# The order of the side work in a diffusion transformer step: new tables for a kernel on one core, with DMA transposes kept apart from GpSimd transfers

## The chip, the cores and the metric

The kernel runs on one core of a Trainium2 chip. The time is that of one execution on the device in microseconds, the median of 3 runs; beside it stands one profiled execution with its trace. The engines are named as in the profile: PE (matmuls), PEld (their weight loads), DVE (VectorE), ACT (ScalarE), POOL (GpSimd) and SP (SyncE, which here only issues DMAs).

## The reference

One layer of a hybrid diffusion backbone, for two groups of 128 tokens (context tokens and latent tokens), in float32 with d = 2048 and a hidden width of 8192:

```
sh1, sc1, g1, sh2, sc2, g2 = split(silu(cond) @ w_ada + b_ada, 6)
h  = rms_norm(x) * (1 + sc1) + sh1
qa, ka, va, qb, kb, vb, ga, gb = split(h @ w_in)
oa = window attention (qa, ka, va);  ob = neighbourhood attention (qb, kb, vb)
x  = x + g1 * ((sigmoid(ga) * (oa @ w_br_a) + sigmoid(gb) * (ob @ w_br_b)) @ w_out)
h2 = rms_norm(x) * (1 + sc2) + sh2
x  = x + g2 * (relu(h2 @ w_up) ** 2 @ w_down)
```

The new keys and values are outputs too. Both groups use the same weights, so each weight tile is multiplied with two sets of 128 tokens (s = 0 and 1).

## The kernel before, in words

**Steps.** The work of PE is a list of 456 steps. A step takes one weight tile of 128x1024 float32 (512 KB) and does 12 matmuls of 512 columns with it. A float32 product is made of three: a value is split into a high part, rounded to the matmul's format, and a low part, the rest; the three products are high x high, low x high and high x low (lines 323 to 325, 434 to 436, 1117 to 1119, 1295 to 1297). The steps in order: 72 for the first projections (q, k, v of both mixers), 64 for the two gates, 32 for the branches (w_br_a and w_br_b, `br_unit`), 32 for w_out (`out_unit`; the last of its four units, out unit 3, is `split_unit`, lines 1089 and on), 16 for the first two units of w_up, and then 7 times 16 steps of w_up in pairs (`up_pair`, steps x and y, with sums of two tiles in place of a part of the products) and 16 of w_down for each pair (`down_unit`).

**What happens to a weight tile.** SP loads it into `raw` (line 231). ACT rounds it to `wH` (`copy`, line 103). DVE subtracts, `wL = raw - wH` (line 265). For the steps listed in `LO_DMA` the low part is made without DVE: ACT writes -wH into `wL` (line 271), and POOL issues a DMA that reads the tile from memory once more and adds it there (line 272, an accumulating transfer). In the pair steps the same is done for `XL`.

**Side work.** Beside that the engines do:

- *Dots* (`dot`, line 1522): the columns of the modulation and of the gates, as products of a row of w_ada with the condition, summed along the row, on DVE. There are 288 such instructions of 128x1024, each followed by a short read-out of its sum; the rows `aT` are loaded by SP (line 1509).
- *Attention*: 8 jobs of logits, softmax and products. Line 891 is the low part of an attention output.
- *Transposes by DMA*: the merged branches m (units 0 to 2) and the activations a of w_up. ACT parts the float32 tile into two planes of 16 bits (`part`, `plm`, `pla`), SP issues a DMA transpose (`flip`, line 953, to `pTm`, `pTa`), ACT puts the planes together (`join`, `fTm`, `fTa`) and rounds (`m2H`, `a15H`), and DVE subtracts (`m2L`, line 976). Unit 3 of m is transposed on PE (`m3H`, `m3L`, line 933).
- *Residuals* (`resid`, lines 1067 and 1068), running sums of w_down (`dsum`, brought back into the accumulators by ACT, `acc<-dsum`, at the start of a unit), and the rows of the gates.

**What sets the order.** Nothing is scheduled by a planner when the kernel is built: the program is written out step by step (`run`, line 293 and on), and each engine works through its own instructions in the order of the program. Tables say at which step each piece of side work is written: `RUN` (a digit for each step: how many steps ahead loads are issued on SP beyond their own lead of 4 steps), `HIA` and `LOOK` (how many steps ahead of PE a tile is rounded and subtracted), `LO_DMA`, `DOTS1`, `DOTS` and `DOTS2` (the steps of the dots), `POST` and `JOBS` (the projections' post-processing and the attention), `M_AT` (for m: the steps after a branch unit at which it is parted, flipped and joined), `U_AT` (the nine pieces of work on each activation a), and some smaller ones. The loop of `run`:

```
while loads and loads[0][0] <= st["i"] + int(RUN[st["i"]]):
    loads.pop(0)[2]()
...
to = st["i"] + int(LOOK[st["i"]]) + 1
while by_dma and by_dma[0] < to + LO_AHEAD:
    ...
    lo_dma(wsteps[by_dma.pop(0)])
prep_to(to, int(HIA[st["i"]]))
st["mm"](st)
```

Of the kernel before, what the change touches and what calls it, by code (L numbers as in the profile page):

```python
# [41 lines left out]
GATE_BACK = 6  # L42
SEED_IN = {3: -1, 4: 0}
SEED_N = (1, 2, 3)
HIA = "334344422101100011100000000122301011111222111222166947553425111013333021221100230021210000200214411000472412200014311212000122441111340010000000100122421210000000000001112224211011355330120500215121100112110022235222103132111122441101022101040213137010043200000101443744564163220000103331003200200112443223211311333897310001332111426411523212022201234110234223000000000021732332243121010110011213659743433000051332322214785182125200100010143210114545247413"
JOIN_LO = 0
SEED_AT = 3
LATE = [1, 0, 0]
ROW_AT = [5, 7, 9, 5]
DIRECT = (3,)  # L50
LO_DMA = [61, 64, 67, 72, 77, 86, 91, 97, 103, 106, 107, 113, 123, 125, 132, 140, 152, 154, 158, 172, 177, 184, 189, 193, 197, 201, 202, 204, 215, 218, 222, 224, 226, 228, 230, 239, 247, 260, 278, 288, 292, 294, 302, 305, 309, 328, 342, 348, 354, 356, 362, 365, 368, 371, 376, 382, 386, 390, 406, 414, 418, 425, 435, 446, 448, 449]
LO_AHEAD = 2

LOOK = "611111122363415244252311332123001130322324232612423111125313141113103124074704401120241642343511333310300011222612060000014948241210105200123253889630426264732454425776691438524821000552257766731000423585037723000160012257691101111014410471447943352966841121000121002032123342233698754699677424411101024267483385777010270111001021431214537842533637352231110241333343187810360357244476465534430140000167275946725442541264301421633233599410002355000466876767"
RUN = "121456457242233512302534211343337663233346434536220000101365356572666431264421250221316831178776544354000102511343588636956330015435499665668999887888323637578788887648731488478895889530499775199482898837126887976459874624247999999989999999999999978377888242565341101001446688446069336899993237667668533532789985978888888888888889987999988889898688615227566656714569888889886476735635451169947788986689998899999999999987898787999999856889995561687444265000"
CONST_AT = [47, 44, 82, 62, 99, 93]
ADA_AT = [None, 5, 13, 22, 24, 38]
XS_AT = {1: 11, 2: 1, 3: 23}
POST = {('kvA', 0): [56, 63, 78], ('qA', 0): [54, 58, 69], ('qA', 1): [67, 70, 79], ('kB', 0): [68, 70, 76], ('qB', 0): [74, 85, 95], ('kB', 1): [86, 104, 106], ('qB', 1): [98, 98, 105]}
JOBS = [[84, 85, 85, 90, 102], [81, 83, 84, 98, 111], [82, 89, 95, 102, 111], [86, 98, 106, 109, 111], [103, 105, 109, 116, 122], [103, 104, 108, 110, 123], [108, 109, 116, 124, 128], [113, 113, 116, 124, 127]]  # L60
SS_AT = [74, 74, 128, 139]
T_AT = [3, 4]
PREP_IN = [5, 7]
DOTS = [49, 51, 52, 52, 53, 56, 57, 57, 59, 59, 61, 63, 66, 69, 69, 70, 70, 77, 80, 80, 81, 82, 82, 83, 83, 85, 85, 85, 89, 89, 90, 92, 92, 96, 99, 99, 99, 101, 101, 104, 104, 106, 106, 108, 108, 109, 109, 110, 112, 113, 114, 119, 119, 121, 121, 121, 121, 125, 125, 128, 128, 130, 131, 132, 136, 136, 137, 137, 137, 140, 140, 146, 149, 149, 150, 150, 153, 153, 155, 156, 163, 167, 171, 171, 172, 174, 175, 175, 179, 180, 184, 186, 186, 187, 188, 190]
DOTS2 = [235, 236, 237, 266, 268, 271, 299, 301, 331, 331, 333, 363, 363, 365, 397, 397, 424, 430, 430, 430, 430, 430, 431, 433, 440, 440, 440, 440, 443, 444, 444, 444]
STAT_AT = [4, 2, -1, 8]
U_AT = [[[1, 2, 5, 10, 10, 15, 15, 21, 22], [2, 10, 13, 14, 16, 17, 19, 23, 25]], [[7, 10, 12, 13, 13, 21, 22, 28, 30], [11, 13, 14, 14, 15, 16, 22, 29, 31]], [[6, 7, 9, 9, 11, 26, 28, 28, 30], [13, 22, 22, 22, 22, 31, 33, 33, 33]], [[6, 8, 8, 9, 10, 12, 14, 14, 16], [3, 5, 5, 5, 5, 11, 23, 26, 32]], [[0, 4, 4, 7, 12, 25, 30, 30, 30], [4, 4, 4, 6, 6, 12, 20, 28, 31]], [[2, 2, 2, 2, 2, 16, 25, 26, 28], [2, 9, 9, 9, 11, 21, 24, 31, 32]], [[8, 8, 9, 9, 9, 10, 11, 11, 11], [2, 8, 9, 9, 10, 13, 13, 13, 16]]]
# [12 lines left out]
def tile_hybrid_step(ctx: ExitStack, tc: tile.TileContext, a):  # L80
# [209 lines left out]

    by_dma = sorted(LO_DMA)

    def run():
        loads.sort(key=lambda x: x[:2])
        for st in wsteps:
            while loads and loads[0][0] <= st["i"] + int(RUN[st["i"]]):
                loads.pop(0)[2]()
            for j in sorted(j for j in pre if j <= st["i"]):
                for fn in pre.pop(j):
                    fn()  # L300
            to = st["i"] + int(LOOK[st["i"]]) + 1
            while by_dma and by_dma[0] < to + LO_AHEAD:
# [156 lines left out]
    def mod_pair(f):  # L459

        box, k0 = {}, 2 * f
        i = ADA_AT[f]
        for j in range(2):
# [310 lines left out]

    for u, ps in POST.items():
        nh = 2 if u[0] == "kvA" else 4
# [230 lines left out]
    def br_unit(n):  # L1007
# [195 lines left out]
    def up_unit(n):  # L1203
# [514 lines left out]
```

## Time and profile before

| | |
|---|---|
| median of 3 runs | 1311.11 us (1310.46 to 1311.5) |
| profiled execution | 1309.16 us |
| its span in the trace | 1307.4 us |
| instructions of PE, DVE, ACT, POOL | 6074, 1609, 1364, 130 |
| granted clock of PE over the span | 0.998 |
| read from memory, written | 403.87 MB, 14.99 MB |

The span runs from the first instruction to the last one; 1.8 us of the execution's time lie outside it. A row of a timeline gives start, duration, engine, line, operation, the tile written and the tiles read, the shape, and in square brackets how long the engine stood idle before it and what released it. A matmul's duration is modelled, and matmuls overlap, so their distance is read from the starts.

### The profile page before, as it was taken

The numbers are of one execution on the slowest core, as the hardware profiler recorded it, in microseconds if no ns is written. First come the engines' busy times: TensorE is split into PE (matmuls) and PEld (weight loads), VectorE is DVE, ScalarE is ACT, GpSimd is POOL, SyncE is SP. The second block draws the span as 40 slices with busy tenths as digits, with TensorE's granted clock in tenths as the row PEclk, the third lists the DMA queues.
The fourth block names the chain that finished last, engine by engine and source line by source line (L and its number), as shares of the span: only waits on it lengthen the run. The fifth ranks groups of instructions, "written<-read, shape, count | busy, mean of one in ns | idle before, by whom it ended". The sixth has DMA issues, their size and how long they took to land.

```text
span 1307.4 us, 18070 instructions
## 1 busy us (share of the span) xinstructions
PE 1286.4 (98%) x6074; PEld 1044.6 (80%) x6074; DVE 1216.4 (93%) x1609; ACT 963.6 (74%) x1364; POOL 107.7 (8%) x130
## 2 busy tenths in 40 slices
PE   8999999999999999999999999999999999999998
PEld 4777788888878888877887887888888888888876
DVE  4589999989999999899789999999999989999997
ACT  5534778967857555655888887898889888888771
POOL 0000002202300000000101000000000010010010
PEclk9999999999999999999999999999999999999999
DMA  9999999999999999999599979899899899999995
GB/s 371 408 409 409 405 363 346 375 335 385 273 367 355 379 378 348 312 360 376 156 271 288 379 238 357 240 330 341 272 351 238 306 305 297 341 279 337 395 321 193
DMA packets 158572, 431.07 MB, mean 330 GB/s; under 512 B 53088, under 2 KB 54352, under 8 KB 158480
## 3 DMA queue, kind: packets, MB, share of 16 engines
q1 hardware_dynamic: 145264, 383.39, 79.5%
q0 software_dynamic: 13024, 46.44, 16.8%
q8 instruction: 47, 0.77, 0.2%
q14 instruction: 45, 0.37, 0.1%
q10 hardware_dynamic: 192, 0.10, 0.0%
HBM read 403.87 MB, written 14.99 MB: 320 GB/s over the span
## 4 chain that ended last, share of the span: by engine, by line
PE 74%; DMA 14%; DVE 6%; ACT 4%; issue 2%; ACTq 0%; DVEq 0%; SPq 0%
PE acc L324 12%; PE acc L323 12%; PE acc L325 12%; PE Q L1296 5%; PE Q L1297 5%; PE Q L1295 5%; PE acc L434 5%; PE acc L435 5%; PE acc L436 5%; DMA raw<-in_w_out 3%; DMA aT<-in_w_adaT 3%; DMA raw<-in_w_in 2%; DMA araw<-in_w_pair 1%; PE ps_ada L340 1%; DVE wL L265 1%
## 5 line engine op out<-in xcount | busy, mean ns | idle before, releaser
L103 ACT ACTIVATE wH<-raw 128x1024 fp32r<-128x1024 f32 (+1 forms) x347 | 347.5, 1044 | 105.8 <-DMA raw<-in_w_in 27.9
L265 DVE TENSOR_TENSOR wL<-raw,wH 128x1024 fp32r<-128x1024 f32 x294 | 346.1, 1220 | 11.1 <-ACT wH L103 10.2
L434 PE MATMUL acc<-wH,hH 128*128 128x512 f32 x276 | 108.7, 394 | 0.7 <-ACT u_qB L103 0.7
L435 PE MATMUL acc<-wL,hH 128*128 128x512 f32 x276 | 107.6, 390 | 0.0
L436 PE MATMUL acc<-wH,hL 128*128 128x512 f32 x276 | 107.5, 389 | 0.0
L323 PE MATMUL acc<-wH,hH 128*128 128x512 f32 x256 | 102.3, 399 | 0.0
L325 PE MATMUL acc<-wH,hL 128*128 128x512 f32 x256 | 99.8, 390 | 0.0
L324 PE MATMUL acc<-wL,hH 128*128 128x512 f32 x256 | 99.8, 390 | 0.0
L1522 DVE CUSTOM_DVE_ANT_0 junk<-aT,cB,cols 128x1024 uint8<-128x1024 f32 x72 | 92.5, 1285 | 0.9
L1522 DVE CUSTOM_DVE_ANT_0 aT<-aT,cB,cols 128x1024 f32<-128x1024 f32 x72 | 91.3, 1294 | 0.3
L103 ACT ACTIVATE uH<-raw 128x1024 fp32r<-128x1024 f32 x56 | 58.9, 1052 | 17.8 <-DVE raw L1367 14.1
L1361 DVE TENSOR_TENSOR t<-raw 128x1024 f32<-128x1024 f32 x56 | 68.2, 1217 | 3.4 <-PE acc L324 3.4
L1373 DVE TENSOR_TENSOR tL<-t,tH 128x1024 fp32r<-128x1024 f32 x56 | 68.2, 1218 | 2.5 <-ACT tH L103 2.1
L1373 DVE TENSOR_TENSOR uL<-raw,uH 128x1024 fp32r<-128x1024 f32 x56 | 68.2, 1217 | 0.2
L103 ACT ACTIVATE XH<-raw 128x1024 fp32r<-128x1024 f32 x56 | 58.7, 1050 | 7.1 <-DVE uL L1373 2.6
L103 ACT ACTIVATE tH<-t 128x1024 fp32r<-128x1024 f32 x56 | 58.8, 1049 | 6.5 <-DVE t L1361 3.3
L434 PEld LDWEIGHTS acc<-wH,hH 128*128 128x128 f32 x276 | 51.8, 188 | 13.7 <-issue 2.1
L436 PEld LDWEIGHTS acc<-wH,hL 128*128 128x128 f32 x276 | 51.8, 188 | 10.9
L435 PEld LDWEIGHTS acc<-wL,hH 128*128 128x128 f32 x276 | 51.8, 188 | 10.7 <-DVE wL L265 0.3
L325 PEld LDWEIGHTS acc<-wH,hL 128*128 128x128 f32 x256 | 48.1, 188 | 10.1
L323 PEld LDWEIGHTS acc<-wH,hH 128*128 128x128 f32 x256 | 48.1, 188 | 9.5 <-issue 0.2
L324 PEld LDWEIGHTS acc<-wL,hH 128*128 128x128 f32 x256 | 48.2, 188 | 9.4 <-DVE scT L1522 0.2
(668 smaller groups left out, 3476.0 us busy)
## 6 DMA issues: line engine op xcount, KB each, us to landing
raw<-in_w_in SPq DMA_DIRECT2D x133, 512.0 KB, 10.2
raw<-in_w_down SPq DMA_DIRECT2D x128, 512.0 KB, 10.2
raw<-in_w_upF SPq DMA_DIRECT2D x112, 512.0 KB, 6.2
aT<-in_w_adaT SPq DMA_DIRECT2D x80, 512.0 KB, 10.2
aT<-in_w_gT SPq DMA_DIRECT2D x64, 512.0 KB, 10.2
araw<-in_w_pair SPq DMA_DIRECT2D x48, 512.0 KB, 10.2
raw<-in_w_out SPq DMA_DIRECT2D x32, 512.0 KB, 10.8
XL<-in_w_upF POOLq DMA_DIRECT2D x19, 512.0 KB, 8.8
```

The source lines that it names most:

```text
L103: act.activation(out, in_, AF.Copy)
L265: dve.tensor_tensor(st["lo"], st["raw"], st["hi"].bitcast(F32), op=OP.subtract)
L323: pe.matmul(acc[tb], sh, wh[:, k, :], start=f, stop=False, **kw)
L324: pe.matmul(acc[tb], sh, wl[:, k, :], start=False, stop=False, **kw)
L325: pe.matmul(acc[tb], sl, wh[:, k, :], start=False, stop=l, **kw)
L434: pe.matmul(acc[tb], sh, wh[:, k, :], start=kt == 0 and k == 0 and not held and not seeded, stop=False, **kw)
L435: pe.matmul(acc[tb], sh, wl[:, k, :], start=False, stop=False, **kw)
L436: pe.matmul(acc[tb], sl, wh[:, k, :], start=False, stop=last and k == 1 and not hold, **kw)
L1295: pe.matmul(acc, stat[0], hi, start=f, stop=False)
L1361: dve.tensor_tensor(t.rearrange("p (a n) -> p a n", a=2), X.rearrange("p (a n) -> p a n", a=2), Y[:, 0:512].unsqueeze(1).to_broadcast([P, ...
L1373: dve.tensor_tensor(b[n + "L"], v, b[n + "H"].bitcast(F32), op=OP.subtract)
L1522: dve.tensor_tensor_reduce(out, box["raw"], cB[s, tag], 1.0, dst if second else baT[:, part, fb:fb + 1], OP.mult, OP.add, dst)
```

## The change

The change alters tables alone; no function and no line of the code behind them. Line 36 (`DOTS1`), line 45 (`HIA`), line 51 (`LO_DMA`, 65 entries where there were 66) and lines between 54 and 74 hold new numbers. A cut of the diff:

```diff
-DOTS1 = [12, 12, 19, 21, 21, 24, 27, 28, 32, 32, 34, 37, 37, 38, 38, 40]
+DOTS1 = [16, 17, 17, 19, 21, 27, 28, 32, 33, 34, 34, 38, 38, 38, 40, 40]
...
-M_AT = [1, 6, 9]
+M_AT = [2, 6, 10]
 FLIP = 2
-P_UP = [3, 0]
+P_UP = [2, 0]
...
-STAT_AT = [4, 2, -1, 8]
+STAT_AT = [2, 0, -1, 8]
```

`HIA`, `LOOK`, `RUN`, `LO_DMA`, `DOTS`, `DOTS2`, `POST`, `JOBS`, `CONST_AT`, `ADA_AT`, `XS_AT` and `U_AT` are replaced as a whole. Over the program PE has the same instructions in the same order. The subtractions of wL on DVE go from 294 to 297 and those of XL from 37 to 35; the accumulating transfers for wL of w_br_a go from 2 to 3, of w_br_b from 2 to 1, of w_out from 6 to 5, of w_down from 18 to 17, of w_up from 4 to 3, and those for XL from 19 to 21. The digits of `RUN` for steps 20 to 59 sum to 55, where they summed to 122; ahead of PE's 400th matmul SP issues 93 loads of 512 KB, where it issued 113.

Three places in the program. The first is DVE's order from the last line of branch unit 3 (line 1017 adds the two branches) to the low part of m unit 3, `m3L`. `ISA` at line 1522 is a dot, and the one-column `ISA` behind it reads out its sum. Before:

```order
L1017 TENSOR_TENSOR g_gA_4473<-g_gA_4473,g_gB_4936 128x512
L1522 ISA junk,scT_158<-aT,cB_3603,scT_158 128x1024
L1522 ISA scT_158 128x1
L265 TENSOR_TENSOR wL<-raw,wH 128x1024
L1522 ISA aT,scT_158<-aT,cB_3605,scT_158 128x1024
L1522 ISA scT_158 128x1
L976 TENSOR_TENSOR m2L<-fTm_5261,m2H 128x1024
L265 TENSOR_TENSOR wL<-raw,wH 128x1024 x3
L933 TENSOR_TENSOR m3L<-ps_T,m3H 128x4x128 x2
```

The same place on DVE now, from the same line 1017 on:

```order
L1017 TENSOR_TENSOR g_gA_4492<-g_gA_4492,g_gB_4940 128x512
L265 TENSOR_TENSOR wL<-raw,wH 128x1024
L976 TENSOR_TENSOR m2L<-fTm_5271,m2H 128x1024
L933 TENSOR_TENSOR m3L<-ps_T,m3H 128x4x128 x2
L265 TENSOR_TENSOR wL<-raw,wH 128x1024
L1522 ISA junk,shT_157<-aT,cB_3357,shT_157 128x1024
```

Two dots and three subtractions fewer stand between the branch unit's end and `m3L`; `m2L` has two dots fewer ahead of it.

The second place is DVE's order late in out unit 2, at its residual (lines 1067 and 1068, `g_2` is the gate and `x_2` the running x of this unit). The tile wL that stands behind the residual before belongs to out unit 3:

```order
L1522 ISA junk,scT_158<-aT,cB_3603,scT_158 128x1024
L1522 ISA scT_158 128x1
L1067 TENSOR_TENSOR t<-g_2_5479,acc 128x512
L1068 TENSOR_TENSOR x_2_4887<-x_2_4887,t 128x512
L1067 TENSOR_TENSOR t<-g_2_5479,acc 128x512
L1068 TENSOR_TENSOR x_2_4887<-x_2_4887,t 128x512
L1522 ISA aT,scT_158<-aT,cB_3605,scT_158 128x1024
L1522 ISA scT_158 128x1
L265 TENSOR_TENSOR wL<-raw,wH 128x1024 x2
```

The residual of out unit 2 on DVE now, with what stands ahead of it:

```order
L265 TENSOR_TENSOR wL<-raw,wH 128x1024
L1522 ISA aT,shT_157<-aT,cB_3359,shT_157 128x1024
L1522 ISA shT_157 128x1
L1522 ISA junk,scT_158<-aT,cB_3357,scT_158 128x1024
L1522 ISA scT_158 128x1
L1067 TENSOR_TENSOR t<-g_2_5476,acc 128x512
L1068 TENSOR_TENSOR x_2_4875<-x_2_4875,t 128x512
L1067 TENSOR_TENSOR t<-g_2_5476,acc 128x512
L1068 TENSOR_TENSOR x_2_4875<-x_2_4875,t 128x512
```

The same tile's wL is now made ahead of the residual and of two dots.

The third place is ACT's order at the start of the last units of w_down: the activations of units 14 and 15 of w_up are joined (`fTa`) and rounded (`a14H`, `a15H`), and the sums so far are copied into the accumulators (`acc<-dsum`). Before:

```order
L103 ACTIVATE acc<-dsum_10922 128x512 x2
L103 ACTIVATE wH<-raw 128x1024
L103 ACTIVATE fTa_11572<-pTa_11546 128x2x512 x2
L103 ACTIVATE a14H<-fTa_11572 128x1024
L103 ACTIVATE dsum_11626<-acc 128x512 x2
L103 ACTIVATE fTa_11647<-pTa_11574 128x2x512 x2
L103 ACTIVATE a15H<-fTa_11647 128x1024
L103 ACTIVATE acc<-dsum_6936 128x512 x2
```

The same place on ACT now:

```order
L103 ACTIVATE acc<-dsum_10917 128x512 x2
L103 ACTIVATE wH<-raw 128x1024 x2
L103 ACTIVATE fTa_11588<-pTa_11541 128x2x512 x2
L103 ACTIVATE a14H<-fTa_11588 128x1024
L103 ACTIVATE dsum_11624<-acc 128x512 x2
L103 ACTIVATE fTa_11641<-pTa_11543 128x2x512
L103 ACTIVATE acc<-dsum_6945 128x512 x2
L103 ACTIVATE dsum_11671<-acc 128x512 x2
L103 ACTIVATE fTa_11641<-pTa_11543 128x2x512
L103 ACTIVATE a15H<-fTa_11641 128x1024
```

The second half of unit 15's join and its rounding have moved behind the copies into the accumulators, and one more rounding of a weight tile stands ahead.

More of the change, by code (lines that the diff above doesn't have):

```diff
@@ L44 @@
 SEED_N = (1, 2, 3)
-HIA = "334344422101100011100000000122301011111222111222166947553425111013333021221100230021210000200214411000472412200014311212000122441111340010000000100122421210000000000001112224211011355330120500215121100112110022235222103132111122441101022101040213137010043200000101443744564163220000103331003200200112443223211311333897310001332111426411523212022201234110234223000000000021732332243121010110011213659743433000051332322214785182125200100010143210114545247413"
+HIA = "001212220310102113100001210001100012133414312347213667640200000004600001000320473311554222331525515435463425300014421235010000005113000005420012000010000000000000000000000021012212665204021532102641311112210323522242361341141053142223200055003214247021257544122343211113683341000145743332210121441325661014430110444887520000000111114340573232253312001013343333222210001001500002230111000224010178677845355300000003423221200315161210000002001124354264556544"
 JOIN_LO = 0
@@ L50 @@
 DIRECT = (3,)
-LO_DMA = [61, 64, 67, 72, 77, 86, 91, 97, 103, 106, 107, 113, 123, 125, 132, 140, 152, 154, 158, 172, 177, 184, 189, 193, 197, 201, 202, 204, 215, 218, 222, 224, 226, 228, 230, 239, 247, 260, 278, 288, 292, 294, 302, 305, 309, 328, 342, 348, 354, 356, 362, 365, 368, 371, 376, 382, 386, 390, 406, 414, 418, 425, 435, 446, 448, 449]
+LO_DMA = [54, 64, 77, 81, 90, 96, 98, 104, 106, 107, 113, 115, 125, 126, 134, 137, 147, 154, 167, 179, 193, 195, 197, 199, 202, 203, 215, 216, 220, 222, 224, 226, 228, 230, 235, 242, 248, 252, 271, 277, 280, 294, 297, 302, 312, 316, 328, 335, 340, 346, 354, 356, 370, 382, 386, 390, 393, 397, 403, 408, 418, 434, 438, 448, 449]
@@ L52 @@
 LO_AHEAD = 2
-LOOK = "611111122363415244252311332123001130322324232612423111125313141113103124074704401120241642343511333310300011222612060000014948241210105200123253889630426264732454425776691438524821000552257766731000423585037723000160012257691101111014410471447943352966841121000121002032123342233698754699677424411101024267483385777010270111001021431214537842533637352231110241333343187810360357244476465534430140000167275946725442541264301421633233599410002355000466876767"
-RUN = "121456457242233512302534211343337663233346434536220000101365356572666431264421250221316831178776544354000102511343588636956330015435499665668999887888323637578788887648731488478895889530499775199482898837126887976459874624247999999989999999999999978377888242565341101001446688446069336899993237667668533532789985978888888888888889987999988889898688615227566656714569888889886476735635451169947788986689998899999999999987898787999999856889995561687444265000"
@@ L56 @@
[L56 to L60, printed above, removed]
+LOOK = "320122121112425413003123131135113254310254350030712111112489598342112325488911310001241110220222620000300000133400492100202426272442137656655964688684888655653375207130430225548804351610138881841040342174117523461045214446120432245411630040106853042961221010000201202222102552542682111475746010001224011275268574765000072101111321216724428800000406300034322212447772056830563557354369716120300331113174563712714401401033133311121375789630000046530676935775"
@@ new lines @@
+RUN = "535358982521111211111000000030102324221111112122111110400652246572543003264232120122432752120112142152010012210035788736651103254942768867787999998987232212799999975115897587998887988775789998987770031443789698865239899876766555766886999623766758875434952511611133325753488988557066786888855675457768777795999985878788788878868488887888988699988672200555565048944929988999999987899999887876245789999999999384555456235656556714366470168961004152442522213555"
+CONST_AT = [44, 56, 80, 86, 104, 86]
@@ L61 @@
+ADA_AT = [None, 5, 13, 20, 24, 38]
+XS_AT = {1: 14, 2: 2, 3: 23}
+POST = {('kvA', 0): [54, 57, 78], ('qA', 0): [54, 59, 66], ('qA', 1): [62, 70, 79], ('kB', 0): [71, 71, 79], ('qB', 0): [75, 82, 91], ('kB', 1): [89, 101, 104], ('qB', 1): [82, 87, 106]}
+JOBS = [[81, 85, 87, 93, 102], [82, 84, 88, 97, 111], [80, 86, 97, 103, 112], [88, 98, 103, 109, 111], [103, 103, 106, 115, 122], [105, 105, 108, 109, 126], [108, 108, 119, 123, 126], [113, 114, 117, 121, 125]]
 SS_AT = [74, 74, 128, 139]
@@ L63 @@
 PREP_IN = [5, 7]
-DOTS = [49, 51, 52, 52, 53, 56, 57, 57, 59, 59, 61, 63, 66, 69, 69, 70, 70, 77, 80, 80, 81, 82, 82, 83, 83, 85, 85, 85, 89, 89, 90, 92, 92, 96, 99, 99, 99, 101, 101, 104, 104, 106, 106, 108, 108, 109, 109, 110, 112, 113, 114, 119, 119, 121, 121, 121, 121, 125, 125, 128, 128, 130, 131, 132, 136, 136, 137, 137, 137, 140, 140, 146, 149, 149, 150, 150, 153, 153, 155, 156, 163, 167, 171, 171, 172, 174, 175, 175, 179, 180, 184, 186, 186, 187, 188, 190]
-DOTS2 = [235, 236, 237, 266, 268, 271, 299, 301, 331, 331, 333, 363, 363, 365, 397, 397, 424, 430, 430, 430, 430, 430, 431, 433, 440, 440, 440, 440, 443, 444, 444, 444]
-STAT_AT = [4, 2, -1, 8]
-U_AT = [[[1, 2, 5, 10, 10, 15, 15, 21, 22], [2, 10, 13, 14, 16, 17, 19, 23, 25]], [[7, 10, 12, 13, 13, 21, 22, 28, 30], [11, 13, 14, 14, 15, 16, 22, 29, 31]], [[6, 7, 9, 9, 11, 26, 28, 28, 30], [13, 22, 22, 22, 22, 31, 33, 33, 33]], [[6, 8, 8, 9, 10, 12, 14, 14, 16], [3, 5, 5, 5, 5, 11, 23, 26, 32]], [[0, 4, 4, 7, 12, 25, 30, 30, 30], [4, 4, 4, 6, 6, 12, 20, 28, 31]], [[2, 2, 2, 2, 2, 16, 25, 26, 28], [2, 9, 9, 9, 11, 21, 24, 31, 32]], [[8, 8, 9, 9, 9, 10, 11, 11, 11], [2, 8, 9, 9, 10, 13, 13, 13, 16]]]
+DOTS = [46, 52, 53, 55, 56, 56, 57, 58, 61, 65, 65, 65, 68, 70, 70, 70, 70, 75, 75, 75, 77, 78, 79, 82, 84, 85, 87, 88, 89, 92, 92, 92, 94, 95, 95, 95, 101, 101, 101, 103, 104, 104, 107, 108, 108, 109, 110, 110, 110, 111, 112, 113, 117, 120, 120, 121, 123, 124, 124, 124, 132, 132, 132, 132, 132, 133, 133, 134, 140, 143, 143, 145, 145, 150, 150, 156, 156, 156, 156, 159, 162, 163, 171, 172, 173, 175, 179, 179, 186, 186, 186, 187, 188, 188, 189, 190]
+DOTS2 = [235, 237, 238, 264, 269, 270, 301, 301, 330, 331, 333, 361, 367, 371, 393, 397, 424, 425, 428, 433, 433, 433, 433, 433, 439, 439, 441, 441, 441, 442, 444, 444]
+STAT_AT = [2, 0, -1, 8]
+U_AT = [[[3, 3, 3, 5, 9, 20, 20, 21, 22], [14, 14, 15, 15, 16, 20, 20, 30, 30]], [[2, 5, 5, 5, 16, 16, 18, 29, 29], [11, 13, 14, 14, 14, 26, 26, 27, 27]], [[9, 10, 10, 10, 11, 15, 29, 30, 30], [12, 17, 21, 21, 21, 29, 33, 33, 33]], [[4, 7, 7, 8, 9, 10, 11, 12, 13], [2, 3, 4, 4, 8, 9, 25, 29, 31]], [[0, 4, 4, 10, 10, 21, 21, 23, 24], [3, 3, 5, 5, 9, 24, 30, 31, 31]], [[3, 9, 9, 10, 10, 26, 28, 29, 29], [8, 10, 11, 12, 12, 21, 25, 32, 32]], [[0, 5, 9, 9, 9, 10, 12, 12, 13], [0, 0, 7, 7, 9, 13, 15, 16, 16]]]
 XLO_IN = True
```

## The prediction

> **What bounds the kernel now.** I read the page first, then the busy times by stage, then what the matmuls waited for.
>
> ```profile
> span 1307.4 us, 18070 instructions
> ...
> PE 1286.4 (98%) x6074; PEld 1044.6 (80%) x6074; DVE 1216.4 (93%) x1609; ACT 963.6 (74%) x1364; POOL 107.7 (8%) x130
> ```
>
> PE is busy for all but 21 us, and the change takes no matmul away. So the time can only move by PE's idle time, by its clock, and by new waits. The stages (columns: length, busy time of PE, PEld, DVE, ACT and POOL, granted clock, DMA share, GB/s):
>
> ```profile
> 60.00:320.00 260.00, 260.00 (x1387) 211.11 (x1386) 247.90 (x372) 174.61 (x355) 26.77 (x23) 1.00 1.00 378
> 400.00:600.00 200.00, 198.86 (x908) 164.41 (x907) 193.93 (x264) 121.80 (x138) 9.49 (x11) 1.00 1.04 356
> 600.00:640.00 40.00, 36.94 (x165) 30.22 (x164) 33.30 (x55) 24.43 (x38) 6.04 (x6) 0.96 0.90 287
> 640.00:1240.00 600.00, 598.01 (x2641) 492.99 (x2640) 575.62 (x670) 513.17 (x596) 42.53 (x56) 1.00 0.95 304
> ```
>
> From 60 to 600 us DVE is full (248 of 260, 194 of 200) and so are the DMA engines. The one stage in which PE loses time is 600 to 640. The list of PE's waits names it (us in all, times, longest):
>
> ```profile
> PE acc L1118 <- DVE wL L265: 3.1, 1, 3.1
> PE acc L323 <- ACT acc L103: 1.7, 1, 1.7
> ...
> PE Q L1296 <- DVE tL L1373: 1.5, 2, 0.8
> ...
> PE acc L324 <- DVE wL L265: 1.0, 2, 0.7
> ```
>
> The longest wait is at L1118, in out unit 3, for a low part wL. PE's timeline there:
>
> ```profile
> 619.18 0.50 PE L1118 MATMUL acc<-wL,m3H 128*128 128x512 f32 x1 [3.06 <-DVE wL L265]
> ...
> 620.09 0.63 PE L1118 MATMUL acc<-wL,m3H 128*128 128x512 f32 x1
> 620.52 0.63 PE L1119 MATMUL acc<-wH,m3L 128*128 128x512 f32 x1
> ```
>
> PE was ready at 619.18 - 3.06 = 616.1. After the wait its matmuls start 0.43 us apart, against 600 / 2641 = 0.23 in the pair stage. The clock of 0.96 over 40 us puts a price on that: 0.04 x 40 = 1.6 us, of which I count 1.5.
>
> Why was DVE late? It has no slack before 600 us, yet it stood idle in one place, from 541 to 559 us:
>
> ```profile
> DVE wL L265 <- ACT wH L103: 2.7, 2, 2.2
> DVE m2L L976 <- ACT m2H L103: 0.9, 1, 0.9
> DVE m3L L933 <- ACT m3H L103: 0.6, 1, 0.6
> ```
>
> That is 4.2 us. ACT was itself held, by the third DMA transpose of m, whose join waited 4.72 us against 2.47 at the second:
>
> ```profile
> 517.21 2.59 ACT L103 ACTIVATE fTm<-pTm 128x1024 uint16<-128x1024 uint16 x2 [2.47 <-DMA pTm<-plm]
> ...
> 545.47 2.59 ACT L103 ACTIVATE fTm<-pTm 128x1024 uint16<-128x1024 uint16 x2 [4.72 <-DMA pTm<-plm]
> ```
>
> On SP's queue the second and the third transpose were issued at (start, length of the issue):
>
> ```profile
> 508.36 6.77 SPq L953 DMA_TRANSPOSE pTm<-plm  x1
> ...
> 529.30 9.25 SPq L953 DMA_TRANSPOSE pTm<-plm  x1
> ```
>
> The second landed at 517.2, 2.1 us after its issue ended (515.1). The third ended its issue at 538.55 and landed at 545.4, 6.9 us later. The DMA issues from 530 to 546 us (KB, us to landing):
>
> ```profile
> wL<-in_w_out POOLq DMA_DIRECT2D x1, 512.0 KB, 9.0
> pTm<-plm SPq DMA_TRANSPOSE x1, 16.1
> ```
>
> With the issue of that POOL transfer
>
> ```profile
> 536.36 0.88 POOL L272 DMA_DIRECT2D wL<-in_w_out  x1 [40.26 <-ACT wL L271]
> ```
>
> both land together, at 536.36 + 9.0 = 529.30 + 16.1 = 545.4. The transpose's data waited out the accumulating transfer.
>
> **The change part by part.** PE keeps the same instructions in the same order. The list of accumulating transfers has 65 entries for 66, which costs DVE one more subtraction (1.2 us) in a program where it has 24 us of slack after 640 us: counted at nothing. If that cover is gone it costs its 1.2.
>
> *The wait in out unit 3.* Prices on DVE come from these rows (612.84 to 614.05 is a dot, 1.21 with its read-out; then a residual pair, 0.68 + 0.69 = 1.37):
>
> ```profile
> 612.84 1.28 DVE L1522 CUSTOM_DVE_ANT_0 junk<-aT,cB,scT 128x1024 uint8<-128x1024 f32 x1
> 614.05 0.08 DVE L1522 DVE_READ_ACCUMULATOR2_ANT scT<- 128x1 f32 x1
> 614.05 0.68 DVE L1067 TENSOR_TENSOR t<-g,acc 128x512 f32<-128x512 f32 x1
> 614.77 0.69 DVE L1068 TENSOR_TENSOR x<-x,t 128x512 f32<-128x512 f32 x1
> ```
>
> and, at the attention (four subtractions in 4.63 us, 1.16 each; three L891 in 1.88),
>
> ```profile
> 377.30 4.63 DVE L265 TENSOR_TENSOR wL<-raw,wH 128x1024 fp32r<-128x1024 f32 x4
> ...
> 383.05 1.88 DVE L891 TENSOR_TENSOR oLA<-ps_o,oHA 128x512 fp32r<-128x512 f32 x3
> ```
>
> Between the last L1017 of branch unit 3 and the wL that PE waited for, DVE's order had 30 dots, 20 subtractions and 6 residual pairs. It now has 25, 23 and 4: -5 x 1.21 + 3 x 1.16 - 2 x 1.37 = -5.3 us. Ahead of that place stand two dots more and one subtraction fewer, +1.3. So wL lands at 619.2 - 4.0 = 615.2 if DVE's 4.2 idle stays, and at 611.0 if it goes. In the new order no accumulating transfer stands within two steps of the third flip, and the first and the second have one 0.6 step ahead and 1.2 steps behind them (a step is 12 matmuls, 2.7 us), so I take the idle as mostly gone. PE is ready at 616.1, or 615.1 once the next item is gained. The wait goes: -3.1, and the clock's 1.5 with it. Next late is nothing on PE's list before the last stage.
>
> [...] The landings above say that a transpose waits out a POOL transfer: 6.9 us for 2.1. [...]
>
> *The two L324 waits* (1.0 together) are for wL tiles that in the new order have 6 fewer dots and 5 fewer dots ahead in their stretch, over 6 us each: -1.0.
>
> *The start of the last down units.* PE waits 1.7 us at L323 for ACT's seeds of the accumulators. On ACT, ahead of those copies, stood
>
> ```profile
> 1254.30 2.58 ACT L103 ACTIVATE fTa<-pTa 128x1024 uint16<-128x1024 uint16 x2
> 1256.91 1.06 ACT L103 ACTIVATE a15H<-fTa 128x1024 fp32r<-128x1024 f32 x1
> ```
>
> Half of the first (1.29) and the second (1.06) now stand behind them, and one more rounding of the second's shape (1.06) stands ahead: 1.29 + 1.06 - 1.06 = 1.3 of the 1.7 gained. Bounds 0 (a later transpose) and 1.7.
>
> *The attention.* At 390.49 PE uses the third of the four wL of 377.30, ready at 380.8:
>
> ```profile
> 390.49 0.39 PE L324 MATMUL acc<-wL,hH 128*128 128x512 f32 x1
> ```
>
> Ahead of it stand now 8 dots and three L891 more: 8 x 1.21 + 1.88 = 11.6, so it is ready at 392.4, 1.9 late. An earlier tile comes out about 1 late by the same count. DVE's dots wait for their own loads, so some of them will not be ahead in time: I take +1.0, between 0 and 2.9.
>
> *The pair stage.* Its two waits at L1296 (1.5) have two DVE instructions fewer ahead at one, the same at the other, and other places lose by a like amount: 0, between -1.5 and +1.5.
>
> Sum: -3.1 - 1.5 - 1.0 - 1.3 + 1.0 + 0 = -5.9 us, on the profiled execution's 1309.16 (span 1307.4 and 1.8 around it): 1303.3. The median of the runs, 1311.11, lies 2.0 above that execution; the same 5.9 off it gives **1305.2**.
>
> **The rivals.** About 0.2%, 2.6 us, is what can be told from no change here: faster is below 1308.5, slower above 1313.7.
>
> [...] Chance 0.12.
>
> *The transposes still collide.* The accumulate behind the second flip may run into its data, and ACT has about half as much work of its own left over the third transpose as before. If the idle doubles by another 4.2, wL lands at 615.2 + 4.2 = 619.4, PE waits 4.3, and the clock drops again: 1305.2 + 4.3 + 1.5 = 1311.0, no change to be measured. Chance 0.21.
>
> *Loads come too late: slower.* The look-ahead of the loads over steps 20 to 59 sums to 55 for 122, so on the mean 67 / 40 = 1.7 steps later; ahead of the 400th matmul SP issues 93 loads of 512 KB for 113. The DMA share of 1.00 from 60 to 320 us leaves no room to catch up. The price lies between 1.7 x 2.7 = 4.6 us and 20 loads at 378 GB/s, 20 x 1.4 = 28. I take one landing
>
> ```profile
> raw<-in_w_in SPq DMA_DIRECT2D x133, 512.0 KB, 10.2
> ```
>
> of 10.2 us, after which ACT and DVE follow PE late up to 600 us: 1315.4. It decides from a loss of 8.5 on (1313.7 - 1305.2); below that it is the second rival's verdict. For it: DVE is full there too, so a late tile cannot be made up. Against: PE lost nothing in 260 us, busy 260.00, with many tiles ahead. Chance 0.17.
>
> **How the numbers follow.** My forecast has 0.50. With the first rival, faster is 0.62; same is 0.21, slower 0.17. Lower end: all of the quoted waits and the clock gone, 3.1 + 1.7 + 1.5 + 1.0 + 1.6 = 8.9, gives 1302.2, less the 1.0 by which the three runs differ: 1301.2, say 1301. Upper end: past the second rival to 1313.7, the point at which the third decides; its 0.17 and some 0.03 below are left out.
>
> **What would show it.** Right: the wait at L1118 gone with the clock at 1.00 from 600 to 640 us; each transpose of m landing 2 to 3 us after its issue; DVE idle under 1.5 us at the branch units' end; the wait at the last down units near 0.4; one or two short waits for wL near 390 us. Wrong: PE idle between 60 and 400 us behind wH that waits for raw (the third rival); a transpose that lands with a POOL transfer (the second); a wait at L1118 in spite of short transposes.

## The result, and the profile after

| | before | after |
|---|---|---|
| median | 1311.16 us (1304.27 to 1311.5, 6 runs) | 1298.88 us (1298.26 to 1299.88, 6 runs) |
| profiled execution, span | 1309.16, 1307.4 | 1298.26, 1296.4 |

The ratio is 0.9916 (0.9896 to 0.9936). The forecast was 1305.2, with a range from 1301.0 to 1313.7: the way was right, and the gain of 12.3 us was twice the one that was forecast and beyond the range.

The page after, and the list of PE's waits from 60 us on (its first rows; the columns are us in all, times, longest):

```profile
span 1296.4 us, 18038 instructions
...
PE 1283.7 (99%) x6074; PEld 1043.7 (81%) x6074; DVE 1215.9 (94%) x1610; ACT 962.4 (74%) x1363; POOL 104.1 (8%) x129
```

```profile
PE Q L1296 <- DVE uL L1373: 0.8, 1, 0.8
PE ps_h L1153 <- DVE h2f L1145: 0.6, 1, 0.6
PE acc L323 <- ACT acc L103: 0.5, 1, 0.5
PE ps_PT L858 <- ACT prob L836: 0.5, 1, 0.5
```

The wait at L1118 (3.1) and the two at L324 (1.0) are gone, and no wait after 60 us is longer than 0.8. The busy times by stage, with the columns of the prediction's table:

```profile
60.00:320.00 260.00, 260.00 (x1387) 211.01 (x1386) 252.44 (x380) 181.48 (x381) 25.61 (x23) 1.00 0.99 371
400.00:600.00 200.00, 200.00 (x918) 166.42 (x917) 198.16 (x268) 122.64 (x142) 9.49 (x11) 1.00 1.03 358
600.00:640.00 40.00, 39.41 (x191) 32.74 (x190) 35.64 (x64) 28.41 (x49) 5.57 (x5) 1.00 0.92 292
640.00:1240.00 600.00, 598.91 (x2637) 493.83 (x2636) 575.28 (x665) 511.54 (x589) 44.38 (x57) 1.00 0.95 306
```

The reader is to compare DVE's column with the one before. From 400 to 600 us it went from 193.93 to 198.16: the 4.2 us of idle time are gone, as forecast. But from 60 to 320 us it also went up, from 247.90 to 252.44. DVE did 4.5 us more of its work there, while PE was busy for all 260.00 us both times. So the tile that PE had waited for at 619.18 was made far ahead of its use: DVE has it done at 605.53 + 1.2 = 606.7, and PE takes it at 611.41.

```profile
605.53 1.22 DVE L265 TENSOR_TENSOR wL<-raw,wH 128x1024 fp32r<-128x1024 f32 x1
```

```profile
611.41 0.39 PE L1118 MATMUL acc<-wL,m3H 128*128 128x512 f32 x1
```

Matmul for matmul (there are 5304 of the large ones, in the same order) PE's lead over the kernel before grows as follows: 1.3 us by the first projections (matmul 640), 2.3 behind the attention (1548), 4.5 before out unit 3, 7.8 at the wait of L1118 and 9.5 behind the slow clock that followed it, 8.7 at the start of the pairs (2400), 9.7 before the end (4100), 11.6 at the last down units (5112) and 11.0 at the end.

### The profile page after: what moved, and what is told of

Read it like the earlier page. It is cut to its first block, busy times and chain, and to the rows that moved or that the text cites. A ratio compares the mean times of both kernels' runs of the same rounds, so it can differ in the third digit from the quotient of the medians.

```text
span 1296.4 us, 18038 instructions
## 1 busy us (share of the span) xinstructions
PE 1283.7 (99%) x6074; PEld 1043.7 (81%) x6074; DVE 1215.9 (94%) x1610; ACT 962.4 (74%) x1363; POOL 104.1 (8%) x129
## 4 chain that ended last, share of the span: by engine, by line
PE 80%; DVE 8%; DMA 5%; ACT 5%; issue 2%; POOL 0%; DVEq 0%; SPq 0%; ACTq 0%
PE acc L323 15%; PE acc L324 15%; PE acc L325 15%; PE Q L1296 5%; PE Q L1297 5%; PE Q L1295 5%; PE acc L434 5%; PE acc L436 5%; PE acc L435 5%; DVE wL L265 1%; DMA araw<-in_w_pair 1%; DVE aT L1522 1%; DVE junk L1522 1%; PE ps_ada L340 1%; DMA raw<-in_w_down 1%
## 5 line engine op out<-in xcount | busy, mean ns | idle before, releaser
L324 PE MATMUL acc<-wL,hH 128*128 128x512 f32 x256 | 100.1, 391 | 0.3 <-DMA wL<-in_w_in 0.3
L103 ACT ACTIVATE XH<-raw 128x1024 fp32r<-128x1024 f32 x56 | 58.8, 1051 | 10.2 <-PE acc L324 5.3
L324 PEld LDWEIGHTS acc<-wL,hH 128*128 128x128 f32 x256 | 48.1, 188 | 11.0 <-DMA wL<-in_w_in 0.9
## 6 DMA issues: line engine op xcount, KB each, us to landing
raw<-in_w_in SPq DMA_DIRECT2D x133, 512.0 KB, 10.2
raw<-in_w_down SPq DMA_DIRECT2D x128, 512.0 KB, 10.2
aT<-in_w_gT SPq DMA_DIRECT2D x64, 512.0 KB, 10.2
araw<-in_w_pair SPq DMA_DIRECT2D x48, 512.0 KB, 10.2
```

Of the source, the lines that this page charges most:

```text
L103: act.activation(out, in_, AF.Copy)
L324: pe.matmul(acc[tb], sh, wl[:, k, :], start=False, stop=False, **kw)
```

## The experiments

Three questions: do the clear transposes make the gain (e1, e8, e13, e14), does one table (e2 to e4), and which part of the program does (e5 to e7, e10, e11). Two more (e9, e12) put a wait in, to see what follows it. The kernel before was run beside each; its medians there were 1307.5 to 1309.2.

**e1: two transfers moved off the transposes of m.**

```diff
 LO_DMA of before
-..., 154, 158, 172, 177, ...
+..., 154, 161, 168, 177, ...
```

> The kernel before, with two accumulating transfers moved in the list: the entry 158 becomes 161 and 172 becomes 168, so that neither is written between a flip of m and its join; nothing else changes, and DVE has the same number of subtractions. Theory of the forecast (a transpose's data waits out a POOL transfer): the first and the third transpose of m land 2 to 3 us after their issue ends (5.1 and 6.9 before), DVE's idle time from 541 to 559 us falls from 4.2 to under 1.5, the wait of 3.1 at L1118 falls under 0.5 and the clock stays at 1.00 from 600 to 640 us: 1306 to 1307. Rival (the transfers have no part in it): the landings stay above 5 us, the wait stays near 3, 1311.

1309.95 (ratio 1.0013, 0.9996 to 1.0029). The waits of PE and of DVE (470 to 620 us):

```profile
PE acc L1118 <- DVE wL L265: 2.9, 1, 2.9
```

```profile
DVE wL L265 <- ACT wH L103: 3.5, 2, 2.0
DVE m3L L933 <- ACT m3H L103: 0.6, 1, 0.6
```

The transposes' landings changed: they came 2.0, 3.6 and 2.1 us behind the end of the issue, where they had come 5.1, 2.0 and 6.8 behind it. So the first step of the theory held. ACT's wait for the third transpose fell from 4.72 to 0.86, but that for the second grew from 2.47 to 7.36. The idle time of 4.1 and the wait of 2.9 did not change: the rival was right on these, not on the landings. The moved transfers still lay beside the issue of two transposes; e13 mends that.

**e2, e3, e4: one table alone.** Each is the kernel before with the tables of after named here.

```diff
 e2: HIA, LOOK    e3: RUN, CONST_AT    e4: DOTS
```

> The kernel before, with the new HIA and LOOK alone (how far ahead of PE tiles are rounded and subtracted). By the order, DVE has 5.5 us less work ahead of the tile that PE waits for at L1118, 10.9 and 2.7 us less ahead of the two at L324, and 9.7 us more ahead of the one at the attention that is used at 390 us. Theory (DVE's order alone is enough, whatever the transposes do): all three waits go, 3.1 + 1.0 and 1.5 of clock: 1305 to 1306. Rival (what counts is the clear transposes, or the dots): the wait at L1118 stays above 2 us, 1309 to 1311. Rival (the tables only work together): longer waits at the attention or elsewhere, 1312 or more.

> The kernel before, with the new RUN (how far ahead loads are issued) and CONST_AT (without which the new RUN meets a tile too late). Third rival of the forecast (later loads starve PE between 60 and 400 us): 4.6 to 28 us longer, 1316 or more, with waits of ACT for raw behind PE's. Theory now, from the trace after: the loads of steps 20 to 59 have slack, so nothing is lost there; the new first digits move loads of w_in ahead of the second block of araw, and the start gains what the trace after shows by the 72nd matmul, 1.2 to 1.6 us: 1309.5 to 1310.5.

> The kernel before, with the new DOTS alone. By the order DVE has 5.5 us less ahead of each of the two tiles waited for at L324 (0.34 and 0.67 us), and the same work as before ahead of the one waited for at L1118. Theory (waits on one full engine are not summed: PE arrives earlier and waits longer at the next): the two waits at L324 go, the one at L1118 grows from 3.1 to about 4.1, 1311. The forecast's sum, taken item by item: 1.0 gained, 1310.1. Rival (dots set the pace up to out unit 3): the wait at L1118 shrinks, 1307 or less.

All three are far slower: e2 1367.76 (1.0457, 1.0422 to 1.0491), e3 1353.98 (1.0351, 1.0324 to 1.0377), e4 1354.99 (1.0357, 1.0328 to 1.0387). PE's longest lists, of e2, e3 and e4:

```profile
PE acc L324 <- DVE wL L265: 18.6, 9, 5.5
PE Q L1295 <- ACT uH L103: 5.4, 1, 5.4
```

```profile
PE acc L323 <- ACT acc L103: 14.1, 2, 12.4
PE acc L434 <- ACT u_qB L103: 9.6, 1, 9.6
```

```profile
PE acc L324 <- DVE wL L265: 14.0, 7, 3.8
PE acc L1118 <- DVE wL L265: 5.0, 1, 5.0
```

e2's last rival holds: the tables work as a set. e3 is slower, as the forecast's third rival had it. e4's wait at L1118 grew to 5.0, but not as its theory said: PE came there 44.6 us later than in the kernel before, not earlier. In all three the losses elsewhere are many times larger than any of the expected ones. Counting DVE's work ahead of one tile, as the prediction did, misses that a changed place in the program makes other instructions wait. For the loads e3 says one thing: with the new RUN PE was still busy for 260.00 of the 260 us from 60 to 320; what it lost, it lost before (9.6) and behind. So the third rival's stage was not the one that starves.

**e5, e6, e7: all tables, for a part of the program.** The tables are cut at steps 126 and 206.

```diff
 e5: steps 0 to 125 of after, the rest of before
 e6: steps 126 to 205 of after, the rest of before
 e7: steps 206 to 455 of after, the rest of before
```

> The kernel before, with every new table up to step 126 (start, first projections, attention, most of the gates) and the old ones from there on. Theory (DVE is full and sets the pace up to out unit 3, so what PE gains ahead of it is given back there): PE is about 2.3 us earlier at its 1500th matmul, as in the trace after, and the wait at L1118 grows from 3.1 to 5.4, or to 6.6 with the one subtraction that DVE has more ahead of it; no faster than before, span 1307 to 1309. Forecast (the new order loses 1.0 at the attention): PE 1.0 later there. Rival (gains add up): span 1305 with a wait at L1118 near 3.

> The kernel before, with every new table from step 126 to 206 (last gates, branches, w_out: dots, look-ahead, loads, transfers, M_AT) and the old ones before and behind. Theory: this holds the gain of the branches and out units: the waits at L324 and L1118 go, the clock stays at 1.00 from 600 to 640 us, DVE's idle time at the branches' end goes, PE is 6 to 7 us earlier at its 2400th matmul, span 1300 to 1301.5. Rival (the room that the later loads and earlier roundings of the front make is needed): the wait at L1118 stays above 1.5 us, span 1304 or more.

> The kernel before, with the old tables up to step 206 and the new ones from there (P_UP, STAT_AT, U_AT, DOTS2 and the rest): the pairs and the end alone. Theory: the wait for the accumulators at the start of the last down units falls from 1.7 to about 0.5, the pairs gain some 0.5; the wait at L1118 stays 3.1: span 1305 to 1306. Forecast's term: 1.3 at the end, 0 in the pairs, 1306.1. Rival (the tail's gain needs the earlier arrival): no change, 1307 to 1308.

e5: 1306.88 (0.9995, 0.998 to 1.0011), span 1302.9. e6: 1308.49 (0.9998, 0.9984 to 1.0012), span 1308.2. e7: 1305.65 (0.9986, 0.9968 to 1.0004), span 1306.5. No one part can be told from no change by its median; the traces say why. In e5, stage and wait:

```profile
60.00:320.00 260.00, 260.00 (x1388) 211.21 (x1387) 252.43 (x379) 182.67 (x382) 28.27 (x23) 1.00 0.99 371
```

```profile
PE acc L1118 <- DVE wL L265: 3.0, 1, 3.0
```

PE is 2.3 us earlier at matmul 1548, and the wait did not grow: DVE is earlier too (252.43 of 260, as in after), and makes the tile at 616.2 instead of 619.1. (No slow clock followed the wait in this one execution; the median of e5 shows no gain.) My theory that it would be given back fell, and so did the forecast's loss at the attention. In e6:

```profile
PE acc L323 <- ACT acc L103: 2.6, 1, 2.6
PE ps_h L1153 <- DVE h2f L1145: 2.3, 1, 2.3
```

The wait at L1118 is gone (the tile is ready at 613.1), but PE now waits 2.3 for h2f, and its lead of 3.4 us over before at L1118 is back to 0.8 by matmul 2400: the next late thing made by DVE, 13 us on, and a slow clock behind it. e7 went as the theory said in the trace, 1.5 earlier at the start of the last down units (0.9 at the end) with the wait at L1118 still 3.0.

**e8: the old M_AT in the changed kernel.**

```diff
-M_AT = [2, 6, 10]
+M_AT = [1, 6, 9]
```

> The changed kernel with the old M_AT = [1, 6, 9]: each plane copy of m is written a step sooner and each join a step sooner, so that ACT meets its wait for the transposes one step (2.7 us) earlier. Theory (the wL of the branches and out units are 4 to 10 us ahead of PE in the trace after, so a stall of ACT is absorbed): ACT's waits for pTm grow by 2 to 6 us, PE loses under 0.5, 1298.5 to 1299.5. Rival of the forecast (it is the room given to the transposes that gains): DVE is idle for 2 to 4 us at the branches' end and the wait at L1118 is back with 1 to 3 us, 1300 to 1303.

1299.59 against before at 1307.64 (0.9931, 0.9912 to 0.9951), span 1296.4 as in after, and no wait at L1118. The theory holds: the step of room that the new M_AT gives is not needed. The transfers stayed where the change had put them, and the transposes landed 2.0 to 2.1 us behind their issue as in after, so e8 does not tell whether clear transposes are needed.

**e10, e11: after without its front, and without its tail.**

```diff
 e10: steps 0 to 125 of before, the rest of after
 e11: steps 206 to 455 of before, the rest of after
```

> The changed kernel with the old tables up to step 126 (e6 with the new tail). Theory (the front's new order lets DVE do 4.5 us more work from 60 to 320 us, 252.4 for 247.9; without it DVE comes later to everything it makes up to h2f, and the wait that went at L1118 comes back at L1153): the wait for h2f at L1153 is 2 to 3 us, L1118 none, span 1306 to 1307, which is e6 less the 1.5 of the tail. Rival (gains add up, the front is worth 2.4 and the rest stays): span 1298.5 to 1299.5.

> The changed kernel with the old tables from step 206 on. Theory (front and middle together hold what DVE gains; the tail's 1.5 is apart from it): no wait above 1 us before the pairs, PE about 8.5 to 9 us earlier than in the kernel before at its 2400th matmul, the wait of 1.7 at the last down units is back, span 1297.5 to 1299. Rival (the tail's tables are needed for the step into the pairs): a wait of 2 us or more at L1153, span 1301 or more.

e10: 1304.36 (0.9973, 0.9958 to 0.9988), span 1303.7. e11: 1300.92 (0.9938, 0.9913 to 0.9962), span 1298.9. Of e10:

```profile
PE ps_h L1153 <- DVE h2f L1145: 2.1, 1, 2.1
PE acc L324 <- DVE wL L265: 1.8, 2, 1.4
```

e11 went as the theory said. In e10 the wait for h2f is back as expected, but the span is 2.3 below the theory's (the tail gained more on e6 than 1.5, since e6 had a longer wait at the last down units, 2.6). Without the front the span is 7.3 longer, of which 1.7 is a slow clock behind the wait for h2f; by the medians it is 5.5. Both are more than twice the 2.3 that PE gains in the front itself; the rival that gains add up is wrong.

What ties the two parts together is DVE's time at h2f. DVE's work from 60 us up to there is nearly the same in all of these kernels, so h2f starts as late as DVE has stood idle on the way:

| | before | e5 | e6 | e10 | after |
|---|---|---|---|---|---|
| DVE starts h2f at (us) | 627.74 | 623.24 | 625.82 | 624.95 | 619.46 |
| busy from 60 us to there | 544.61 | 545.95 | 545.24 | 545.48 | 547.20 |
| idle from 60 us to there | 23.13 | 17.29 | 20.58 | 19.47 | 12.26 |

The front alone (e5) takes 5.8 of the idle time away, the middle alone (e6) 2.6, and both 10.9.

**e9, e12: a wait put in.** At the seed of the first of the last down units of the changed kernel:

```diff
-    for tb in range(2):
+    for tb in [0] * (k - 1) + [0, 1]:    # k = 7 in e9, 4 in e12
         copy(box["acc"][tb], src[:, tb, :])
```

> The changed kernel with one wait put in: at the start of the first of the last down units ACT copies the first half of the seed seven times instead of once (the same values), 6 copies of about 0.54 us more. PE's wait there grows from 0.5 to 3.7 us; DVE and ACT have time to spare in that stage, so nothing else should follow. Theory (a wait of about 3 us on PE is followed, in some executions, by some us at half the clock, as behind L1118 in the kernel before; that is what spreads that kernel's times over 8 us): 3.2 longer at the least, 1302.1, the executions spread over 3 us or more, those with the longest time at a lower mean clock, median 1302.5 to 1306. Rival (a wait costs its own length; the spread of the kernel before has another cause): 1302.1, spread under 2 us, clock 0.999 to 1.000 in all.

> As e9, with 3 copies more instead of 6: PE's wait there grows from 0.5 to about 2.1 us. Theory (the clock answers to long waits, those of 3 us and not those under 2): 1.6 longer, 1300.5, spread and clock as in the changed kernel or little wider. Rival (any wait draws the clock down in proportion): half of what e9 loses beyond its 3.2, and half of its spread.

The wait in e9:

```profile
1250.34 0.50 PE L323 MATMUL acc<-wH,a14H 128*128 128x512 f32 x1 [2.84 <-ACT acc L103]
```

e9: 1303.59 (0.9959, 0.9944 to 0.9974). One execution of ten took 1301.69 at a mean clock of 1.000, which is 3.4 longer than the profiled one of after, about the copies' own length (at this place PE did not wait at all in after; its 0.5 was at the next unit). The others took 1303.17 to 1305.68 at 0.997 or 0.998. So the wait of some 3 us cost itself and, in nine of ten executions, 1.5 to 4 us more at the lower clock. In the execution shown here no slow clock followed it. e12: 1301.63 (0.9945, 0.9923 to 0.9967); three of five executions at 1.000 (1300.28 to 1301.63) and two at 0.998 (1302.03 and 1302.76). With a wait of 1.9 us the mean clock was lower too, only less often (two of five for nine of ten), against my theory; where it begins was not settled. The 20 executions of before beside these ran from 1304.3 to 1306.74 for the five at 1.000 up to 1313.52 at 0.997.

**e13, e14: no transfer beside a transpose, and the joins later.** Both from the kernel before.

```diff
 e13  LO_DMA: entries 158 and 172 become 141 and 142
 e14 -M_AT = [1, 6, 9]
     +M_AT = [1, 6, 10]
```

> The kernel before, with the two accumulating transfers that met transposes taken out of the branches altogether: entries 158 and 172 become 141 and 142, so that no transfer is issued between the first flip of m and the third join; DVE has as many subtractions ahead of the wait at L1118 as before. (In e1 the moved transfers still lay beside the issue of the second and third transposes.) Theory of the forecast: all three transposes land within 2 to 3 us of their issue's end and within 12 us of its start, DVE's idle time from 541 to 559 us falls from 4.2 to under 1.5, the wait at L1118 from 3.1 to under 1, and 1 to 2 us of it come back at h2f: span 1304 to 1305.5. Rival, which e1 favours (ACT waits for a transpose that takes 9 to 12 us anyway, since the join stands three steps behind the flip): idle time above 3, the wait at L1118 at 2.5 to 3, span 1305 to 1307.5 and no difference in the median.

> The kernel before, with M_AT = [1, 6, 10]: the joins of m one step (2.7 us) later behind the flips, the transfers where they were. Theory (it is the distance from flip to join that leaves ACT, and through it DVE, waiting, not the transfers): ACT's wait for the third pTm falls from 4.7 to 2 or less, DVE's idle time from 541 to 559 us from 4.2 to about 1.5, the wait at L1118 from 3.1 to 0.4 or so, with 1 to 2 us back at h2f: span 1304 to 1305.5. Rival (the idle time follows from the transfers, whatever the distance): idle time above 3, the wait near 3, span 1307.

e13: 1308.65 (1.0011, 1.0001 to 1.0021). The three transposes:

```profile
L953 SPq DMA_TRANSPOSE pTm<-plm x3: 8212/8717/8802, 495.5 to 535.2; - x3
...
DMA to landing us min/median/max: 10.2/10.7/10.8
```

DVE's waits (470 to 620 us) and PE's:

```profile
DVE wL L265 <- ACT wH L103: 6.4, 2, 3.8
```

```profile
PE acc L324 <- DVE wL L265: 2.5, 2, 2.1
...
PE acc L1118 <- DVE wL L265: 1.0, 1, 1.0
```

With no transfer near them the transposes land 10.2 to 10.8 us after their start, against 13.8, 8.8 and 16.1 before, and 2.0 to 2.1 behind the end of their issue, against 5.1, 2.0 and 6.8: the two with a transfer in flight had been held up by 3 to 5 us. The run gains nothing: the same two tiles, made by DMA earlier, let a tile of the branches come 2.1 late, ACT's stall moves, and DVE idles for 6.4. That is at 487 and 491 us, ahead of the first transpose. At the branch units' end, where the forecast had its 4.2, DVE did not idle in e13, and the wait at L1118 fell to 1.0; but DVE came there 6.5 us later than before, so e13 does not show what clear transposes alone are worth. e14: 1315.55 (1.0065, 1.0048 to 1.0082):

```profile
PE acc L323 <- ACT m2H L103: 5.3, 1, 5.3
```

The join a step later comes behind four more roundings on ACT, which waited 6.7 us for their loads of w_out, and m itself is 5.3 us late for PE. Neither side of this question gained by itself; my theory of the distance fell.

## Why the prediction was right or wrong

The terms of the forecast's sum against PE's lead in the traces (minus is a gain, in us):

| part | forecast | traces |
|---|---|---|
| start and front, to matmul 1548 | +1.0 | -2.28 |
| to out unit 3 (the two waits at L324) | -1.0 | -2.27 |
| the wait at L1118 | -3.1 | -3.22 |
| the slow clock behind it | -1.5 | -1.73 |
| h2f, to matmul 2400 | 0 | +0.76 |
| the pairs | 0 | -1.03 |
| the last down units | -1.3 | -1.18 |
| sum | -5.9 | -10.95 |

*The front: the step that failed.* The forecast took "From 60 to 600 us DVE is full (248 of 260, 194 of 200)" and "it stood idle in one place" for granted, and priced the front at a loss of 1.0. The row that it quoted shows 12.1 us in which DVE was idle between 60 and 320 us. In after there are 7.6 of them; PE's 260.00, the same both times, says nothing of that. PE gained 2.3 us up to the end of the attention, 3.3 of the 5.0 by which the sum was short. By e5 and e10 the front is worth these 2.3 and, by what it lets the middle do, 7.3 of the whole in the traces, 5.5 by the medians. The loss forecast at the attention did not come: of the two tiles that it called late, the one used at 390 us came 0.24 us ahead of its use (forecast 1.9 late). The waits at ps_S and ps_PT, left out of the sum, fell from 1.3 + 0.8 to 0.5. At the start a wait of 0.7 for u_qB and some of the first loads' went, 1.3 in all, which the forecast did not price.

*The wait in out unit 3 and its clock.* Right in kind and size for PE. DVE's idle time of 4.2 went. The tile came at 606.7, not between 611.0 and 615.2: the working had DVE 1.3 us later at the end of the branches, and DVE came there 2.5 us earlier (its last line 1017 starts at 541.54, where it started at 544.03).

*The cause given for it.* Its first half holds in these traces: before, the first and the third transpose landed within 0.1 us of an accumulating transfer, 5.1 and 6.8 us behind the end of their issue, and in after, with none in flight at that end, each landed 2.0 to 2.1 us behind it, as the forecast's sign had it. But the idle time did not hang on that. In after ACT waits as long for the third transpose as before (4.72), and DVE does not idle; six roundings follow behind the join without a wait:

```profile
539.10 2.59 ACT L103 ACTIVATE fTm<-pTm 128x1024 uint16<-128x1024 uint16 x2 [4.74 <-DMA pTm<-plm]
...
543.88 5.80 ACT L103 ACTIVATE wH<-raw 128x1024 fp32r<-128x1024 f32 x6
```

Before, 2.7 of DVE's 4.2 us were waits for wH, and these roundings were themselves waiting for loads of w_out, the longest time here:

```profile
550.66 1.06 ACT L103 ACTIVATE wH<-raw 128x1024 fp32r<-128x1024 f32 x1 [1.51 <-DMA raw<-in_w_out]
```

From 546 to 560 us ACT waits for such loads for 2.3 to 5.7 us in all in before, e1, e5, e7, e13 and e14, and not at all in after, e6, e8, e10 and e11. The first have the old tables for steps 126 to 205, but for the entries edited, the others the new ones. That holds without the front too: in e6 DVE idles for 1.8 at that place. Which of these tables does it was not separated (by e2 to e4, a single table loses too much elsewhere to tell), and no run puts the transfers back beside the transposes in the changed kernel. So it stays open whether clear transposes are needed; by e1 and e13 they gained nothing in the kernel before. In this the first rival (clearing the transposes buys nothing, chance 0.12) was right. That the third landing was long for SP's own loads does not hold: without a transfer in flight a transpose landed 2.0 to 2.1 us behind the end of its issue (e13).

*The L324 waits and the end.* The first was right (1.0 forecast; PE's lead grew by 0.5 and 0.8 at the two places). At the end the first of the last down units gained 1.9, its whole wait of 1.7 and a little more, and 0.7 was lost again behind it, 0.5 of that in a wait at the next unit (1.3 forecast; 1.4 at its start in e7). The pairs gained 1.0 against 0.

*From the profile to the median.* The forecast took 5.9 off both. The profiled execution of before lay 2.0 below its median, that of after 0.6 below. The rest of the difference is the spread of the kernel before, and the slow clock is a good part of it: of its 74 executions beside the experiments the 11 at a mean clock of 1.000 have a median of 1306.0, the 36 at 0.998 one of 1308.6 and the 6 at 0.997 one of 1310.3. It is not all, for one execution of e1 took 1311.0 at 1.000. The term of 1.5 was what one execution lost; e9 shows that others lose more, and the traces of e1 and e5 that some lose nothing. Against the medians of before beside the experiments the gain is 8.6 to 10.4 us rather than 12.3, so a part of the 12.3 is chance.

*The range.* Its lower end took the waits that were quoted, 8.9 us. Left out were those at ps_S, ps_PT and u_qB (2.8) and the start.

*The other rivals.* Loads to PE came late nowhere (DMA share 0.99 and PE 260.00 up to 320 us). By 320 us SP had issued 104 loads of weight tiles before and 105 after, so their later place in the program was no later time. The one wait of PE for a DMA behind 60 us in after is 0.3, for an accumulating transfer of w_in. Transposes that collide again were not seen in after.

## What to carry to other kernels

Where PE is busy throughout a stage, look at the engine that feeds it: its idle time there is lead that a later wait, hundreds of microseconds on, is paid from (here 4.5 us more of DVE's work from 60 to 320 us; without it, in e10, PE waited 2.1 us for h2f at L1153, for 0.6 in after). A wait that is removed can uncover the next late product of the same engine (in e6 the wait at L1118 went, and 2.3 us for h2f came 13 us on), so count that engine's lead at the two or three tiles behind it before booking the gain. Tables that set one order belong together: try a stage with all of them rather than one table for all stages (e2 to e4, one table or two for all stages, came out 3.5 to 4.6% slower; e5 to e7, all tables for a stage, within 0.2% of the kernel before).

## What the runs showed of the hardware

A wait of PE of 2 to 3 us often cost more than itself. In e9 nine of ten executions lost a further 1.5 to 4 us at a mean clock of 0.997 to 0.998, and the kernel before, with its wait of 3 us, spread from 1304.3 to 1313.5 where the changed kernel stayed within 1298.26 to 1299.88. In the trace of before the granted clock is 0.50 for 3.41 us at the end of the wait (the columns are those of the stages above; the clock is the third from the right):

```profile
619.82:623.23 3.41, 3.41 (x10) 2.63 (x9) 1.68 (x3) 3.38 (x4) 1.21 (x2) 0.50 1.05 372
```

Such a stretch lies at the end of waits of 3.06 (before), 3.04 (e7, 6.8 us long), 2.33 (e6), 2.10 (e10), 2.12 and 1.99 (both e13); none lies behind 2.97 (e5), 2.87 (e1), 2.84 (e9) and 2.60 (e6). So it comes in some executions and not in others. In four places it followed a wait of only 2.0 to 2.3 us, and with the 1.9 of e12 two of five executions showed a mean clock of 0.998, where the six of after were at 0.999 to 1.000.

A DMA transpose of 512 KB landed 2.0 to 2.1 us behind the end of SP's issue with no accumulating transfer in flight at that end (after, e8, e13 and the second of before), and 5.1 and 6.8 us behind it, within 0.1 us of the transfer's own landing, with one in flight (before). The issue itself took SP 4.8 to 9.6 us in after, 6.8 to 9.3 in before and 8.2 to 8.8 in e13.
